# Two z units from the unnormalised input, convolutions ahead of the norms, and the first head's memory copies in another ring

## The chip, the cores and the metric

The kernel runs on one core of one Trainium2 chip. The metric is the device time of one execution in microseconds (us). Before the change it is 1135.06 us, the median of three runs (1134.79 to 1135.84). The trace and its page come from one further execution under the profiler.

## What is computed

One inference step of a one-layer hybrid encoder, for 512 prompt frames of a new stream and 32 sample frames of a running one (544 columns, T, together). Cut to what matters here:

```python
def _rmsnorm(x, g):
    xf = x.astype(jnp.float32)
    y = xf * lax.rsqrt(jnp.mean(xf * xf, axis=-1, keepdims=True) + EPS)
    return (y * g.astype(jnp.float32)).astype(x.dtype)
...
        xn = _rmsnorm(h, norm_g[l])
        proj = xn @ w_in[l]
        u, v_m, z_m, ig_pre, fg_pre, q_h, f_h, i_h, g_h, ga, gb = jnp.split(proj, _split_points(), axis=-1)
        c, conv_new = _causal_conv(u, conv0[l].astype(u.dtype), conv_w[l], conv_b[l])
        c = jax.nn.silu(c).astype(f32)
        ch = c.reshape(B_, T, M_HEADS, M_HD)
        qm = jnp.einsum('bthd,hde->bhte', ch, w_qm[l].astype(f32))
        km = jnp.einsum('bthd,hde->bhte', ch, w_km[l].astype(f32)) * (M_HD ** -0.5)
        vm = v_m.astype(f32).reshape(B_, T, M_HEADS, M_HD).transpose(0, 2, 1, 3)
        ig = (ig_pre.astype(f32) + b_ig[l].astype(f32)).transpose(0, 2, 1)
        lf = jax.nn.log_sigmoid(fg_pre.astype(f32) + b_fg[l].astype(f32)).transpose(0, 2, 1)
        hm, C_new, n_new, m_new = _mlstm(qm, km, vm, ig, lf, C0[l].astype(f32), n0[l].astype(f32), m0[l].astype(f32))
        hm = _head_layernorm(hm.transpose(0, 2, 1, 3), mnorm_g[l].astype(f32))
        hm = (hm + m_skip[l].astype(f32) * c) * jax.nn.silu(z_m.astype(f32))
        ya = hm.astype(x.dtype) @ w_brm[l]
```

An RMS norm multiplies each frame by one number, r, and each input channel by a gain, g. So a product of the input with g alone, scaled by r per frame afterwards, is the product of the normalised input. The mLSTM has four heads of 512 channels each. Behind it come an HGRN2 branch, a merge and the output, which the change does not touch.

## The kernel before

**Numbers and layout.** Channels lie on the 128 partitions, frames along a row. The input is eight tiles x0 to x7 (line 202), each with its 544 columns and the gain. To keep float32 accuracy, each operand of TensorE is a pair: a high part, rounded to the matmul's format on ScalarE, and a low part, the remainder, by a subtraction on VectorE. A product takes three matmuls (high with high, low with high, high with low). For weights this is `split_piece` (line 127): the raw weight arrives by a DMA on SP's queue into one of eight raw buffers, ScalarE casts the high part (line 132), VectorE or, for some weights, POOL subtracts the low part (line 133).

**Two forms of the input.** `x0` (line 1237) holds the pairs of the input times g, without r; they are made first, for the u products that begin the kernel. `xs` (line 1290) holds the pairs of the normalised input: `norm(k)` multiplies x by g and rb in place on VectorE (line 1286) and casts the high part on ScalarE (1289); `norm_low(k)` subtracts on VectorE (1293). `rb` (1297) is r of every frame, on all partitions.

**The first stage (lines 1215 to 1438).** In this block the order of the instructions on ScalarE, VectorE and TensorE is the order of the program. TensorE runs u (four tiles of the first head, from x0), the gate rows, and then the value product (lines 1333 to 1372): eight steps k of twelve matmuls, into four PSUM banks vp, with vq for the sample frames after the steps 3 and 7. Between these steps stand the norms, the weight splits (`value_weight`), and the scaling of u (`conv_scale`). Behind the loop follow, for each of four tiles, the causal convolution: `conv_first` on ScalarE (646), `conv_rest`, three multiply-adds on VectorE (651), `silu` on ScalarE (657, 658, with the cast 1381) and `silu_low` on VectorE (1386). The result is scaled out of vp by `value_out` (1396, 1397). `stage_gates` (714) is a generator: a bias on ScalarE; then line 725 on VectorE with Exp and Ln on ScalarE; then scans along the rows; then further exponentials.

**The pump and the heads (lines 1439 to 1479).** From here only TensorE's order is written out; the instructions of the other engines are placed by a scheduler, by priority, with the pairs `tc.high_priority()` and `tc.issue_after(...)` to steer it. `Pump` hands out further projections in small steps. For the first head these are four z units of class `One` (347), 32 to 35, of 48 matmuls each, from `xs`; then pairs of u units of the next head (class `Two`, line 404), which also read `xf`, sums and differences of the normalised input made by `xf_sums` (320) and laid into the buffers that `x0` leaves (`pair_tile`, tags x0 and x1; q's pairs use them too). `pump.prepare(n)` asks for the loads and splits of the first n blocks; each z unit has four blocks. The first two z units run ahead of the first head's k (`pump.to(EARLY)`, line 1445), z2 and z3 later. A finished z unit is copied out of PSUM by VectorE and goes through Silu on ScalarE (lines 686 and 688).

For each head: `stage_k`, `stage_q`, `stage_scores`, then `mchain` (952). In it `memory` (910) accumulates one of four blocks of the new memory C in a pair of PSUM banks (there are two pairs in all, `paux`), copies it into a tile Co on ScalarE (929) and writes it to HBM. `sample()` (1036) computes the sample frames' numerators, which VectorE adds up (1047). `new_memory` (1023) updates the running stream's memory.

**The rings of buffers.** Tag "s" (`slot`, line 80) has 22 buffers, tag "e" (`eslot`, line 83) has 12. A tile waits until a buffer of its ring is free, that is, until the last reader of the tile in it is done. Co, the tiles x, ub, z, kf and the old memory c0 are in "e"; scores, weighted keys and convolutions are in "s".

## Time and profile before

| | |
|---|---|
| median of three runs | 1135.06 us |
| the profiled execution: its time | 1135.85 us |
| the profiled execution: span from first to last instruction | 1133.3 us |
| TensorE's mean granted clock over the span | 0.995 of full speed |
| instructions | 23757 |
| DMA | 157.94 MB, mean 139 GB/s |

The page gives, for each engine, its busy time and share of the span (PE is TensorE, PEld its weight loads, DVE VectorE, ACT ScalarE, POOL GpSimd, SP the engine that issues most DMAs). The trace can also be asked for a list of waits (who waited for whom), for a table of stages (busy time, granted clock and DMA in given stretches) and for a timeline of each engine. In a timeline's line stand the start and the duration in us, the engine, the line of the kernel, the operation, what it writes and reads, and how many alike were merged; in brackets, how long the engine was idle before it and what it waited for.

### The profile page before, as it was taken

To read this page: it belongs to the slowest core of one execution; us is meant where nothing else is said; L and a number is where in the kernel's file an instruction comes from. 1 tells how busy PE (TensorE), PEld (TensorE's weight loads), DVE (VectorE), ACT (ScalarE), POOL (GpSimd) and SP (SyncE) were. 2 spreads that over 40 slices of the span, in tenths; PEclk is the share of its full clock that TensorE was granted. 3 is DMA by queue.
4 is the path that set the end of the run, shared out by engine and by line. 5 is a ranking of instruction groups with operands and counts; after the bars stand their busy time and mean duration, and the time that the engine had idled before them with its cause. 6 is when DMAs were issued, how large, how long until landed. Compare 5 with 4: busy or idle time off the path is not lost.

```text
span 1133.3 us, 23757 instructions
## 1 busy us (share of the span) xinstructions
PE 1112.4 (98%) x8733; PEld 1088.1 (96%) x8733; DVE 900.9 (79%) x2040; ACT 669.5 (59%) x1506; POOL 163.7 (14%) x308
## 2 busy tenths in 40 slices
PE   8999899999999999999999999999999999999998
PEld 8888799999999999999999999999999999999998
DVE  6898958778598685986888689999999977654485
ACT  6578436755476463765556367776766667333462
POOL 7113000000020000201100123222332210000000
PEclk9999999999999999999999999999999999999999
DMA  7133223414354232453567666666666685332753
GB/s 226 55 114 105 70 93 113 157 60 124 114 162 164 66 122 103 150 174 100 181 194 210 203 140 141 133 152 152 149 142 152 153 220 151 122 101 79 252 160 117
DMA packets 90140, 157.94 MB, mean 139 GB/s; under 512 B 10149, under 2 KB 17829, under 8 KB 90025
## 3 DMA queue, kind: packets, MB, share of 16 engines
q1 hardware_dynamic: 80352, 139.33, 38.4%
q0 software_dynamic: 8784, 15.99, 9.2%
q8 instruction: 68, 1.11, 0.4%
q10 hardware_dynamic: 888, 1.12, 0.3%
q14 instruction: 48, 0.39, 0.1%
HBM read 131.49 MB, written 24.91 MB: 138 GB/s over the span
## 4 chain that ended last, share of the span: by engine, by line
PE 83%; DVE 5%; DMA 3%; ACT 2%; issue 1%; POOL 0%; ACTq 0%; POOLq 0%; DVEq 0%
PE d L502 34%; PE ya L167 8%; PE yb L167 4%; PE q L167 4%; PE o L167 4%; PE pg L1860 4%; PE k L167 4%; PE C L917 4%; PE sc L877 3%; PE nm L1094 3%; PE pl L1632 2%; DMA ws<-in_w_in 2%; PE ple L167 1%; PE yt L1142 1%; PE ht L1708 1%
## 5 line engine op out<-in xcount | busy, mean ns | idle before, releaser
L420 POOL DMA_DIRECT2D ws<-in_w_in x46 | 40.4, 884 | 237.2 <-DVE hkq L1656 54.9
L516 ACT COPY t<-d 128x272 f32<-128x272 f32 x126 | 47.7, 379 | 8.8 <-PE d L502 8.7
L1656 DVE TENSOR_TENSOR hkq<-hkq,q 128x288 f32<-128x288 f32 (+1 forms) x96 | 40.8, 431 | 2.6 <-PE pl L1640 0.9
L1632 PE MATMUL pl<-hkq,km 128*128 128x128 f32 x224 | 38.0, 292 | 1.1 <-ACT km L1621 0.9
L651 DVE SCALAR_TENSOR_TENSOR cv<-ub,vec,cv 128x547 f32<-128x547 f32 x48 | 37.5, 783 | 0.4
L1029 DVE SCALAR_TENSOR_TENSOR c<-c,wi,Cs 128x258 f32<-128x258 f32 x32 | 15.3, 480 | 25.9 <-PE Cs L1027 25.8
L1632 PEld LDWEIGHTS pl<-hkq,km 128*128 128x128 f32 x224 | 31.1, 189 | 3.2 <-ACT km L1621 2.8
L1621 ACT COPY km<-hkq 128x256 f32<-128x256 f32 x56 | 24.0, 428 | 13.9 <-DVE hkq L1656 4.6
L929 ACT COPY Co<-C 128x258 f32<-128x258 f32 x30 | 9.8, 378 | 34.1 <-PE C L917 24.9
L1172 DVE TENSOR_TENSOR y<-ya,y 128x272 f32<-128x272 f32 x48 | 18.9, 435 | 8.7 <-PE ya L167 8.6
L1663 DVE COPY_PREDICATED at<-lmask,pl 128x256 f32<-128x256 uint8 (+1 forms) x56 | 25.3, 451 | 0.1
L1105 ACT COPY y<-nm 128x516 f32<-128x516 f32 x16 | 9.4, 590 | 23.3 <-PE nm L1094 22.8
L643 POOL COPY uo<-ub 128x3 f32<-128x3 f32 x16 | 17.9, 1116 | 36.1 <-DVE ub L525 27.0
L1082 DVE BATCH_NORM_STATS2 bs<-y 128x6 f32<-128x512 f32 (+1 forms) x20 | 13.8, 690 | 8.8 <-ACT y L1105 8.6
L917 PE MATMUL C<-vhl,kwh 128*128 128x258 f32 x96 | 16.5, 296 | 4.4 <-ACT Co L929 3.8
L1600 POOL TENSOR_SCALAR_AFFINE_SELECT aa<-at 128x128 f32<-128x128 f32 x32 | 19.6, 643 | 8.1 <-DVE at L1663 8.0
L817 POOL COPY vsm<-vt 128x96 f32<-128x96 f32 x12 | 7.3, 608 | 87.7 <-DVE vt L523 45.2
L1094 PE MATMUL nm<-vhl,sh 128*128 128x258 f32 x112 | 18.4, 287 | 1.2 <-ACT y L1105 1.2
L477 POOL DMA_DIRECT2D ws<-in_w_in x15 | 15.2, 1014 | 29.3 <-DVE ws272l L133 23.5
L917 PEld LDWEIGHTS C<-vhl,kwh 128*128 128x128 f32 x96 | 14.0, 201 | 4.7 <-ACT Co L929 4.0
L1847 DVE TENSOR_TENSOR h<-o,h 128x272 f32<-128x272 f32 x16 | 6.3, 436 | 14.5 <-PE o L167 14.5
L1094 PEld LDWEIGHTS nm<-vhl,sh 128*128 128x128 f32 x112 | 15.4, 190 | 2.0 <-ACT y L1105 1.7
(4503 smaller groups left out, 4980.4 us busy)
## 6 DMA issues: line engine op xcount, KB each, us to landing
ws<-in_w_in POOLq DMA_DIRECT2D x61, 256.0 KB, 4.9
ws<-in_w_in SPq DMA_DIRECT2D x46, 256.0 KB, 4.1
ya_d<-y SPq DMA_DIRECT2D x32, 272.0 KB, 2.5
y<-ya_d SPq DMA_DIRECT2D x24, 272.0 KB, 3.4
c<-in_C SPq DMA_DIRECT2D x16, 258.0 KB, 3.8
out_Cs<-c SPq DMA_DIRECT2D x16, 258.0 KB, 2.8
out_Cp<-Co SPq DMA_DIRECT2D x12, 258.0 KB, 2.4
x<-in_xT SPq DMA_DIRECT2D x8, 272.5 KB, 4.7
```

The lines of the kernel that those rows point to most:

```text
L167: PE.matmul(both[b][:m, :TH], part(w, off + k * step, m, x), xx[:, half(b)], start=(k == 0 and j == 0), stop=(k == n - 1 and j == 2),)
L420: G.dma_start(t, w_in[u][:, i * WP : (i + 1) * WP], accum_op=ALU.add)
L502: PE.matmul(ps, ww[:, c], xx, start=(start and k == 0 and j == 0), stop=end, skip_group_check=not start,)
L516: self.kept = S.copy(t, ps)
L651: V.scalar_tensor_tensor(cv[:, :547], ub[:, j : j + 547], vcol(V_CW + 4 * ft + j), cv[:, :547], ALU.mult, ALU.add)
L877: PE.matmul(pn[:, 0, :n], ks[f][x][:, j * P : (j + 1) * P], qs[f][y][:, NS + j * P : T], start=(f == 0 and i == 0), stop=(f == KH - 1 and ...
L917: PE.matmul(pn[g][:, :VH], kw[b][x][:, f * P : (f + 1) * P], vv[b][y][:, g * VH : (g + 1) * VH], start=(b == 0 and j == 0), stop=(b == NB ...
L1094: PE.matmul(pn[:, g, :VH], st[j][x][:, (i - j) * P : (i - j + 1) * P], vv[j][y][:, g * VH : (g + 1) * VH], start=(j == 0 and q == 0), stop ...
L1632: PE.matmul(pn[:, 0, b * P : (b + 1) * P], km[:, b * P : (b + 1) * P], view(qq, b * P, ((2 * c, P // (2 * c)), (HB + c, 2), (1, c))), star ...
L1656: V.tensor_tensor(x, x, d, ALU.mult)
L1663: V.copy_predicated(at[:, :n], lmask[:, li, :n], pn[:, 0, :n])
L1860: PE.matmul(ps, part(w, k * P, P, x), xx[:, c], start=(k == 0 and j == 0), stop=(k == KD - 1 and j == 2))
```

## The change

It has these parts.

- `One` takes an optional source. The first two z units of head 0 read `x0` in place of `xs`, and their eviction multiplies by `rb` in place of copying.
- In the first stage the convolutions (scale, first, rest, silu, low) move to before and into the value product; the norms move behind, the last four to after the value evictions. Each value weight's split keeps its rank among the others. `pump.prepare(1)` and `prepare(3)` move into step 2 of the value product, `prepare(5)` and `(7)` stand between the evictions and the last norms. `st8[0]["last"]`, which holds back `xf_sums(0)` and `(3)`, is now the last `norm_low`.
- `stage_gates` asks for its row tiles when they are first written, not at its start.
- Head 0's Co tiles come from ring "s" in place of "e".
- In head 0's `mchain`, `xf_sums(1)` no longer stands ahead of `sample()`; it is issued behind the sample's last sum, with `xf_sums(2)`.
- The u evictions `conv_in` lose their `issue_after` on POOL.

The definitions of `silu`, `silu_low` and `value_out` stand unchanged further up; their old place is cut.

```diff
--- before.py
+++ after.py
@@ -347,9 +347,9 @@
     class One:
 
 
-        def __init__(self, key, unit, cut, then):
+        def __init__(self, key, unit, cut, then, src=None):
             self.key, self.unit, self.cut, self.then = key, unit, cut, then
-            self.ps = None
+            self.ps, self.src = None, src
 
         def raws(self):
             return [(self.unit, 0), (self.unit, 1)]
@@ -381,7 +381,7 @@
                     self.ps = phalves(f"d{self.unit}")
                 halves = (slice(0, self.cut), slice(self.cut, T))
                 for k in (2 * i, 2 * i + 1):
-                    xh, xl = xs[k]
+                    xh, xl = (self.src or xs)[k]
                     for j, (x, xx) in enumerate(((0, xh), (0, xl), (1, xh))):
                         for b, c in enumerate(halves):
                             PE.matmul(
@@ -683,7 +683,10 @@
             z = eslot(f"z{h}{f}")
             for b in range(2):
                 with tc.high_priority():
-                    out = V.tensor_copy(z[:, b * TH : (b + 1) * TH], acc[b][:, :TH])
+                    if f < 2:
+                        out = V.tensor_tensor(z[:, half(b)], acc[b][:, :TH], rb[:, half(b)], ALU.mult)
+                    else:
+                        out = V.tensor_copy(z[:, half(b)], acc[b][:, :TH])
             st8[h].setdefault("copies", []).append(out)
             act = S.activation(z[:, :T], z[:, :T], AF.Silu)
             st8[h]["z"][f] = (z, act)
@@ -704,7 +707,7 @@
             todo += [pair("v", f, 16 + h * KH + f, lambda f: plain(eslot(f"vt{h}{f}")), value) for f in (0, 2)]
             todo += [pair("z", f, 32 + h * KH + f, lambda f: plain(eslot(f"z{h}{f}")), gate) for f in (0, 2)]
         else:
-            todo += [One(("z", f), 32 + f, TH, lambda acc, f=f: gate_one(f, acc)) for f in range(KH)]
+            todo += [One(("z", f), 32 + f, TH, lambda acc, f=f: gate_one(f, acc), x0 if f < 2 else None) for f in range(KH)]
         if h + 1 < MH:
             st8[h + 1]["ub"] = [None] * KH
             todo += [pair("u", f, (h + 1) * KH + f, inner_tile, inner) for f in (0, 2)]
@@ -713,19 +716,20 @@
 
     def stage_gates(fg, ig):
 
-        e, bl, *rr, m, em = (slot(f"row{i}")[:MH, :T] for i in range(KD))
-        lf = wl = e
-        nm = m
         ct = tp.tile([P, T + NS], F32, tag="bc", name="rst")
         rst = ct[:MH, :T]
         ct = tp.tile([P, T + NS], F32, tag="bc", name="d0")
         d0 = ct[:MH, :T]
         S.activation(fg, fg, AF.Identity, bias=gv[:, 1:2])
         yield
+        e = slot("row0")[:MH, :T]
         V.scalar_tensor_tensor(e, fg, -1.0, fg, ALU.mult, ALU.min)
         S.activation(e, e, AF.Exp)
         S.activation(e, e, AF.Ln, bias=1.0)
         yield
+        bl, *rr, m, em = (slot(f"row{i}")[:MH, :T] for i in range(1, KD))
+        lf = wl = e
+        nm = m
         V.scalar_tensor_tensor(lf, fg, 0.0, e, ALU.min, ALU.subtract)
         G.memset(rst, 1.0)
         G.memset(rst[:, 0:1], 0.0)
@@ -923,7 +927,7 @@
                     )
             if b < NB - 1:
                 yield
-        co = eslot(f"Co{h}{f}")
+        co = (eslot if h else slot)(f"Co{h}{f}")
         with tc.high_priority(), tc.issue_after(after.ins) if after is not None else nullcontext():
             for g in range(2):
                 S.copy(co[:, g * VH : (g + 1) * VH], pn[g][:, :VH])
@@ -1015,9 +1019,6 @@
             lo = slice(NS, 2 * NS)
             with tc.high_priority():
                 low = V.tensor_tensor(vs[lo, :HD], pt[lo, 0, :], vs[lo, :HD].bitcast(F32), ALU.subtract)
-        if h == 0:
-            with tc.issue_after(low.ins):
-                xf[1] = xf_sums(1)
         yield 3
 
         def new_memory(f, g):
@@ -1053,7 +1054,8 @@
             ysm, read, last = sample()
             if h == 0:
                 with tc.issue_after(last.ins):
-                    xf[2] = xf_sums(2)
+                    for k in (1, 2):
+                        xf[k] = xf_sums(k)
             yield 1
         if h == MH - 1:
 
@@ -1264,8 +1266,7 @@
         w3.append(split_piece(raws[1], "wu31", WP, WSPLIT))
         wg = gate_weight(a["w_gate"], "wg")
         products(KD - 1)
-        with tc.issue_after(summed.ins):
-            uin = [conv_in(f, acc[f], False) for f in range(NF)]
+        uin = [conv_in(f, acc[f], False) for f in range(NF)]
         acc.append(phalves("u3"))
         steps(acc[3], w3, range(U3AT))
         pb = paux("r0pb")
@@ -1290,23 +1291,52 @@
             xs.append((xh, xl))
 
         def norm_low(k):
-            V.tensor_tensor(xs[k][1], xt[k][:, :T], xs[k][0].bitcast(F32), ALU.subtract)
+            return V.tensor_tensor(xs[k][1], xt[k][:, :T], xs[k][0].bitcast(F32), ALU.subtract)
+
+        cc, cs, vv0 = [], [], []
+
+        def silu():
+            f = len(cc)
+            cc.append(conv_silu(f, cv[f]))
+            hi, lo = slot(f"cs{f}h", F32R), slot(f"cs{f}l", F32R)
+            S.copy(hi[:, :T], cc[f][:, :T])
+            cs.append((hi, lo))
+
+        def silu_low(f):
+            hi, lo = cs[f]
+            V.tensor_tensor(lo[:, :T], cc[f][:, :T], hi[:, :T].bitcast(F32), ALU.subtract)
+
+        def value_out():
+            b = len(vv0)
+            if b < 2:
+                vhl = sp.tile([P, 2, SLOT], F32R, tag="d", name=f"vhl0{b}", bufs=2)
+                vh, vl = vhl[:, 0], vhl[:, 1]
+            else:
+                vh, vl = eslot(f"vh0{b}", F32R), eslot(f"vl0{b}", F32R)
+            c = r[:, b + 1 : b + 2]
+            S.mul(vh[:, :HD], vp[b], c)
+            V.scalar_tensor_tensor(vl[:, :HD], vp[b], c, vh[:, :HD].bitcast(F32), ALU.mult, ALU.subtract)
+            with tc.issue_after(summed.ins):
+                G.tensor_copy(vh[:, HD:VW], one4)
+                G.tensor_copy(vl[:, HD:VW], zero4)
+            vv0.append((vh, vl))
 
         value_weight()
         value_weight()
         rb = slot("rb")
         S.copy(rb[:, NS:T], pb[:, 0, :])
         S.copy(rb[:, :NS], pb[:, 1, :NS])
-        conv_scale(uin[0])
-        norm(0)
-        norm(1)
+        cv = []
+        for f in range(NF):
+            conv_scale(uin[f])
+            cv.append(conv_first(f, uin[f]))
+        conv_rest(0, uin[0], cv[0])
         value_weight()
-        norm(2)
-        norm_low(0)
-        with tc.issue_after(summed.ins):
-            uin.append(conv_in(3, acc[3], True))
-        value_weight()
-        cv = [conv_first(0, uin[0])]
+        uin.append(conv_in(3, acc[3], True))
+        conv_rest(1, uin[1], cv[1])
+        silu()
+        cv.append(conv_first(3, uin[3]))
+        silu_low(0)
         gp = phalves("gates")
         for k in range(KD):
             both = ((GW + GN, x0[k][0]), (GN, x0[k][1]))
@@ -1319,41 +1349,45 @@
                         start=(k == 0 and m > GN),
                         stop=(k == KD - 1 and m > GN),
                     )
-        norm(3)
-        norm_low(1)
-        norm(4)
         gt = slot("gt")
         for b in range(2):
             S.copy(gt[:GN, half(b)], gp[b][:GN, :TH])
             V.tensor_tensor(gt[:GN, half(b)], gp[b][GW : GW + GN, :TH], gt[:GN, half(b)], ALU.add)
         value_weight()
+        conv_rest(2, uin[2], cv[2])
+        silu()
+        silu_low(1)
+        value_weight()
 
         vp = [pd.tile([P, 512], F32, tag="h", name=f"vp{b}") for b in range(NB)]
         vq = paux("vq")
+        pump = Pump(fill(0))
         for k in range(KD):
             if k == 1:
-                norm(5)
-                norm_low(2)
-                norm_low(3)
-                value_weight()
-                norm(6)
-                norm_low(4)
+                conv_rest(3, uin[3], cv[3])
+                silu()
+                silu_low(2)
+                silu()
                 fg, ig = (slot(n)[:MH, :T] for n in ("fg", "ig"))
                 V.tensor_tensor(fg, gt[0:MH, :T], rb[0:MH, :T], ALU.mult)
                 V.tensor_tensor(ig, gt[32 : 32 + MH, :T], rb[32 : 32 + MH, :T], ALU.mult)
-                norm(7)
+                gates = stage_gates(fg, ig)
+                next(gates)
+                value_weight()
+                silu_low(3)
+                norm(0)
+                norm(1)
             if k == 2:
-                norm_low(5)
                 value_weight()
-                norm_low(6)
-                norm_low(7)
-                conv_scale(uin[1])
-                cv.append(conv_first(1, uin[1]))
-                conv_scale(uin[2])
-                cv.append(conv_first(2, uin[2]))
-            if k == 3:
+                norm_low(0)
+                norm_low(1)
+                norm(2)
                 value_weight()
-                cv.append(conv_first(3, uin[3]))
+                norm(3)
+                norm_low(2)
+                pump.prepare(1)
+                norm_low(3)
+                pump.prepare(3)
             wh, wl = wv[k]
             xh, xl = x0[k]
             three = ((xh, wh), (xl, wh), (xh, wl))
@@ -1371,70 +1405,33 @@
                     i = k + 1 - NB + j
                     PE.matmul(vq[j * NS : (j + 1) * NS, 0, :], xg[:, i], wraw[i], start=(i < NB), stop=(i >= NB))
 
-        cc, cs, vv0 = [], [], []
-        gates = stage_gates(fg, ig)
-
...
-        pump = Pump(fill(0))
-        conv_rest(0, uin[0], cv[0])
-        silu()
-        next(gates)
-        conv_rest(1, uin[1], cv[1])
-        silu_low(0)
-        pump.prepare(1)
-        silu()
-        pump.prepare(3)
         value_out()
         value_out()
-        conv_rest(2, uin[2], cv[2])
-        silu_low(1)
-        silu()
-        conv_rest(3, uin[3], cv[3])
+        norm(4)
         value_out()
         value_out()
-        silu_low(2)
-        silu()
+        norm_low(4)
+        norm(5)
         pump.prepare(5)
-        silu_low(3)
-        pump.prepare(7)
-        st8[0]["wk"] = weight(a["w_km"][0, 0], "wk00", eng=G)
         vsum = slot("vsum")[:NS, :HD]
         S.copy(vsum, vq[:NS, 0, :])
         for j in range(1, NB):
             V.tensor_tensor(vsum, vq[j * NS : (j + 1) * NS, 0, :], vsum, ALU.add)
+        pump.prepare(7)
+        st8[0]["wk"] = weight(a["w_km"][0, 0], "wk00", eng=G)
+        norm_low(5)
         vs0 = small("vs", [3 * NS, VW], F32R, bufs=1)
         for i in (0, 2):
             S.mul(vs0[i * NS : (i + 1) * NS, :HD], vsum, r[:NS, 0:1])
-        st8[0]["last"] = V.scalar_tensor_tensor(
+        V.scalar_tensor_tensor(
             vs0[NS : 2 * NS, :HD], vsum, r[:NS, 0:1], vs0[:NS, :HD].bitcast(F32), ALU.mult, ALU.subtract
         )
         with tc.issue_after(summed.ins):
             G.tensor_copy(vs0[:, HD:VW], vone)
+        norm(6)
+        norm(7)
+        norm_low(6)
+        st8[0]["last"] = norm_low(7)
         next(gates)
     with tc.manual_schedule(engines={mybir.EngineType.PE}):
         for h in range(MH):
```

98 lines of the change are left out of this document (49 added, 49 removed).

## The prediction

> **What bounds the kernel now.** I read the page's busy times first, then the list of TensorE's waits over the first 260 us, then the granted clock around the longest of them, then TensorE's timeline there.
>
> ```profile
> PE 1112.4 (98%) x8733; PEld 1088.1 (96%) x8733; DVE 900.9 (79%) x2040; ACT 669.5 (59%) x1506; POOL 163.7 (14%) x308
> ```
>
> TensorE is busy for 1112.4 of the 1133.3 us of the span. The other engines count only where TensorE waits for them, and at most some 21 us of waiting can be had, beside matmuls that run slowly.
>
> ```profile
> PE C L917 <- ACT Co L929: 3.8, 1, 3.8
> PE d L387 <- ACT wi330h L132: 2.5, 1, 2.5
> PE k L167 <- POOL wk010l L133: 1.3, 1, 1.3
> ...
> PE k L167 <- ACT wk010h L132: 1.0, 1, 1.0
> PE nm L1094 <- ACT y L1105: 0.7, 1, 0.7
> ...
> PE C L917 <- DVE y L1047: 0.5, 1, 0.5
> ```
>
> Columns: total, times, longest. Three places hold 8.6 us: the second z unit (2.5), the second half of head 0's k (1.3 and 1.0), the third block of head 0's new memory (3.8). Each costs more than its wait, since TensorE comes back slow:
>
> ```profile
> 74.00:76.00 2.00, 2.00 (x10) 2.00 (x10) 2.00 (x2) 2.00 (x5) 1.77 (x2) 0.50 0.51 130
> ...
> 90.00:92.00 2.00, 2.00 (x9) 2.00 (x10) 2.00 (x6) 1.20 (x3) 2.00 (x3) 0.50 0.48 131
> ```
>
> The third column from the right is the granted clock. It is 0.50 of full speed for some 2 to 3 us behind each wait. So I take a place's whole loss from the timeline (start, duration, instruction):
>
> ```profile
> 70.25 0.41 PE L387 MATMUL d<-xh,wi321l 128*128 128x272 f32 x2
> 73.16 0.82 PE L387 MATMUL d<-xh,wi330h 128*128 128x272 f32 x2 [2.50 <-ACT wi330h L132]
> ...
> 80.57 0.42 PE L167 MATMUL k<-cs0h,wk000h 128*128 128x272 f32 x2
> ...
> 86.36 0.41 PE L167 MATMUL k<-cs3h,wk001l 128*128 128x272 f32 x2
> 87.82 0.52 PE L167 MATMUL k<-cs0h,wk010h 128*128 128x272 f32 x2 [1.05 <-ACT wk010h L132]
> ...
> 96.97 0.41 PE L167 MATMUL q<-cs0h,wq000h 128*128 128x272 f32 x2
> ```
>
> A pair of matmuls follows the last every 0.25 us, so the first z unit ends at 70.50, and the first half of k takes 80.57 to 86.61: 6.04 us for 48 matmuls without a stall. The second z unit has 48 as well, and is over at 80.57. Place A loses 80.57 - 70.50 - 6.04 = **4.03 us**. Place B, the second half of k, loses 96.97 - 86.61 - 6.04 = **4.32 us**.
>
> ```profile
> 137.07 0.28 PE L1027 MATMUL Cs<-vs,kws 96*128 96x258 f32 x1
> ...
> 140.47 0.65 ACT L929 COPY Co<-C 128x258 f32<-128x258 f32 x2 [0.28 <-DMA out_Cs<-c]
> ...
> 141.17 1.23 PE L917 MATMUL C<-vhl,kwh 128*128 128x258 f32 x4 [3.82 <-ACT Co L929]
> ...
> 145.55 0.28 PE L1027 MATMUL Cs<-vs,kws 96*128 96x258 f32 x1
> 145.67 0.64 PE L917 MATMUL C<-vhl,kwh 128*128 128x258 f32 x4
> ...
> 148.56 0.28 PE L1027 MATMUL Cs<-vs,kws 96*128 96x258 f32 x1
> ```
>
> Here the fourth block of the memory runs 145.67 to 148.68, 3.01 us. The third could start at 137.19 and end at 140.20; it ends at 145.67. Place C loses **5.47 us**. What the third block waits for is a PSUM buffer, emptied by a copy into Co at 140.47, and that copy waited for a buffer of Co: the only free one came when c's write-out had landed.
>
> A rule beside this. The Trainium skill, "TensorE: Matmul & The Clock Gate", section "Part 1: The HAM clock gate", has the clock fall only after an idle window of about 3.4 us. The 2.50 us at place A were enough here, so the trace disagrees, and I follow the trace. By the rule A would be worth 2.50 us instead of 4.03.
>
> **The change part by part.** First, place A. Why is wi330h late? ScalarE's timeline:
>
> ```profile
> 69.43 0.61 ACT L658 ACTIVATE c<-cv 128x512 f32<-128x512 f32 x1
> 71.39 0.66 ACT L688 ACTIVATE z<-z 128x544 f32<-128x544 f32 x1 [1.35 <-DVE z L686]
> 71.96 0.63 ACT L1381 CAST cs3h<-c 128x544 fp32r<-128x544 f32 x1
> 72.49 0.61 ACT L132 CAST wi330h<-wi33r 128x512 fp32r<-128x512 f32 x1
> ```
>
> The first z unit's silu (line 688) stood in the queue ahead of the last convolution's cast and of the second z unit's weight cast. It could only run when the first z unit was finished, so the second unit's weights could never be ready when TensorE wanted them. With the change the first two z units need only x0 (there since the u products) and rb at the eviction, so the order can be turned round: the convolutions go beside the value matmuls, the norms behind. The work is the same; what matters is what stands in front of wi330's two halves. I walk VectorE's new order with these durations:
>
> ```profile
> 42.61 1.36 DVE L1293 TENSOR_TENSOR xl<-x,xh 128x544 fp32r<-128x544 f32 x2
> ...
> 62.52 1.41 DVE L1397 SCALAR_TENSOR_TENSOR vhl<-vp,rms_r,vhl 128x512 fp32r<-128x512 f32 x2
> 63.85 2.43 DVE L651 SCALAR_TENSOR_TENSOR cv<-ub,vec,cv 128x547 f32<-128x547 f32 x3
> ...
> 70.57 0.79 DVE L686 COPY z<-d 128x272 f32<-128x272 f32 x2
> ...
> 80.84 0.71 DVE L725 SCALAR_TENSOR_TENSOR row<-fg 4x544 f32<-4x544 f32 x1
> ```
>
> A norm_low is 0.65, a value eviction 0.7, a conv_rest 2.4, a z eviction 0.8 for both halves; I take a norm as a value eviction, 0.7, a weight's low half 0.65, a cast on ScalarE 0.55. From 30.7 on: three conv_scale, conv_rest 0 and 1, u3's eviction, silu_low 0 and the gate additions end near 40.4; conv_rest 2 and 3, wv3 to wv5's splits, three lows, fg, ig and the first two norms end at 52.3; wv6, wv7, two more norms and wi32's split end at 61.4. The two value evictions then end at 63.7, norm 4 at 64.4, the other two value evictions, held up by ScalarE, which runs norm 4's cast first, at 67.0, norm_low 4 and norm 5 at 68.4. ScalarE casts xh5 and then wi330h by 69.4, VectorE has wi330l by 70.1. TensorE wants them at 70.5 and 71.0. So the wait is gone, with **1 us to spare**; wi331l, behind the three additions into vsum and the z eviction, comes at 73.4 against 74.0. Gain 4.03 us; if the cover of 1 us fails by a little, TensorE loses just that.
>
> What must stay hidden: the value matmuls need wv4 to wv7 at these times.
>
> ```profile
> 51.98 0.72 PE L1362 MATMUL vp<-wv4h,x 128*128 128x512 f32 x2
> ...
> 60.47 0.63 PE L1362 MATMUL vp<-wv7h,x 128*128 128x512 f32 x2
> ```
>
> In the walk wv4 is split by 44.7 and wv7 by 57.8, against 51.98 and 60.47 (2.7 us to spare). The z eviction becomes a multiplication by rb; no row has it. The nearest are the copy above, 0.8 for both halves, and norm's line, 0.7 for a whole row: between a gain of 0.1 and a loss of 0.4 on VectorE, hidden by the unit behind it, whose PSUM halves are others. I take the copy's. The z units' write of x4 and x5's buffers waits for norm_low 4 at most, done at 67.7, and for norm_low 5, at 74.1, against 70.6 and 76.6. Each prepare that moves takes its weight loads along, into SP's queue:
>
> ```profile
> 52.06 0.80 SPq L122 DMA_DIRECT2D wi32r<-in_w_in  x2
> ...
> 60.90 1.95 SPq L122 DMA_DIRECT2D wi34r<-in_w_in  x2
> ```
>
> wi32's waits for raw buffers that the last vq of the first half frees just before 52, wi34's for those of wi32, split by 61.4 in the walk and at 62.4 now. Asked for earlier they go at the same times, in the same order, and nothing behind them moves. POOL's copies of uo come up to 16 us earlier, into idle time of POOL. x0's buffers, which q and the sums xf 0 and 3 take over, stay in use until the second z unit ends at 76.5; the sums stand behind norm_low 7, past 77, and q's first write comes some 15 us later, so nothing waits for them.
>
> Second, place B. The queue in front of wk010h:
>
> ```profile
> 80.82 1.28 ACT L726 ACT_TABLE_LOAD   x1
> 82.11 0.66 ACT L726 ACTIVATE row<-row 4x544 f32<-4x544 f32 x1
> 82.79 1.28 ACT L688 ACT_TABLE_LOAD   x1
> 84.08 0.66 ACT L688 ACTIVATE z<-z 128x544 f32<-128x544 f32 x1
> 84.76 1.28 ACT L727 ACT_TABLE_LOAD   x1
> 86.05 0.66 ACT L727 ACTIVATE row<-row 4x544 f32<-4x544 f32 x1
> ```
>
> Exp, the second z's silu, Ln: three table loads. Their start is line 725 on VectorE, ended at 81.55, 1.0 us after k began. In the new order line 725 follows norm_low 7: my walk ends it at 79.1, or 80.4 if wi34's two low halves come first, while k begins at 76.5. The chain then starts 2.6 to 3.9 us after k instead of 1.0. Against it, silu of z can run before Exp and save a table load and itself (1.9 us), or wk010h itself can run while ScalarE waits. So B changes by a loss of 1.9 us (chain late by 2.9, against the 1.0 that k's eviction would wait anyway) up to a gain of all 4.32. I take **0**, since the two shifts nearly cancel.
>
> Third, place C. Counting head 0's slots of ring "s" from the code: eight of kw, six of scores, four of c are alive when the memory runs, 18 of 22. Four Co fit, so no copy waits for a write-out. The copies take 0.65 us a block, against blocks of 3.01, so the PSUM pair turns over. Gain 5.47 us. Moving xf_sums(1) behind the sample's sums frees VectorE between them: the 0.5 us wait for line 1047 should go too. Its transforms were done before 142 and are first read by the pair behind z3, past 166; cover of 20 us. I leave the 0.7 us wait of nm as it is, with a gain of 0.7 at the low end. C in all: **6.0 us**.
>
> The rest (silu_low, gate rows asked for later, weights of k on POOL) moves work beside busy TensorE, and behind 200 us TensorE hardly waits, so the gain reaches the end whole. Sum: 4.03 + 0 + 6.0 = 10.0. The profiled execution took 1135.85 (span 1133.3, and 2.55 around it), 0.79 above the median: 1135.85 - 10.0 = 1125.8, and by the median **1125.0 us**.
>
> **The rivals.**
> (1) The scheduler again sets the first z's silu ahead of wi330h: 1 us of slip does it. Only C pays: 1129.0. For it: it happened now, at the same point. Against: wi330 stands earlier by a conv and three casts.
> (2) B goes as well, wk010h being cast while ScalarE waits for line 725: 1125.0 - 4.3 - 0.7 = 1120.0. For it: by the walk ScalarE idles there 1 to 2 us. Against: its load waits for raw buffers that come free only then.
> (3) Ring "s" is fuller than my count, and a Co waits for the Co before it, as in ring "e": only A pays, 1131.0.
> (4) The change doesn't do what it says: A's wait moves to wi331 or k, C's stays; 1135.
> (5) Slower: the convolutions stand ahead of the value weights. If VectorE falls more than 3 us behind the walk, every weight from wv4 to wv7 comes late, TensorE starves once a step, and the clock, which fell behind waits of 1.05 and 1.30 at B, stays at 0.50. The stretch 51.98 to 63.4 then takes 11.4 more, and the waits 2: 1125.0 + 13.4 = 1138.4.
> (6) Only idle of a whole window gates the clock; then A pays 2.50 and the time is 1126.5. The row 74 to 76 speaks against it; no chance of its own.
>
> **How the numbers follow.** Forecast 0.47 (1122.5 to 1127.5), (1) 0.16, (2) 0.15, (3) 0.10, (4) 0.07, (5) 0.05. About 0.2%, 2.3 us, is what a measurement of this kernel tells from no change. Faster: 0.47 + 0.16 + 0.15 + 0.10 = 0.88; same 0.07; slower 0.05. The range reaches from (2) to just above (3), 1120.0 to 1131.5, and leaves out 0.12.
>
> **What would show it.** A: no wait of TensorE for wi330h, the clock at 1.00 from 66 to 82, k beginning near 76.5. B: a wait for wk010 of some 2 us remains, and 0.50 behind it. C: Co's copies wait for TensorE alone and the four memory blocks follow every 3.0 us. Wrong would be: waits for wv, a wait for cols or for k's PSUM, or a Co that waits for a DMA.

## The result

The changed kernel takes **1126.65 us** (median of five runs, 1126.06 to 1128.63), beside 1135.06 for the kernel before on the same chip (five runs, 1134.77 to 1137.06): a ratio of 0.9926, 95% interval 0.9912 to 0.9941. That is 8.4 us less, where 10.1 were predicted. The profiled execution took 1126.18 us, its span is 1124.3.

First the list of TensorE's waits over the first 260 us of the kernel after (total, times, longest):

```profile
PE k L167 <- POOL wk011l L133: 2.2, 1, 2.2
...
PE k L167 <- ACT wk011h L132: 1.1, 1, 1.1
PE sc L881 <- ACT q L860: 0.9, 1, 0.9
```

The waits for wi330h (2.5), Co (3.8) and y (0.5 and 0.7) are gone, and so are those for the two parts of wk010 (1.0 and 1.3). In their place stand waits for wk011, the other piece of k's second weight half (1.1 and 2.2, together more than the two of wk010), one for the scores' q, and one for the low part of wi330. Now TensorE's timeline of the kernel after, at the points that divide the stages:

```profile
62.09 0.77 PE L387 MATMUL d<-x,wi320h 128*128 128x272 f32 x4
...
69.74 0.52 PE L387 MATMUL d<-x,wi330l 128*128 128x272 f32 x2 [0.85 <-DVE wi330l L133]
...
75.38 0.41 PE L167 MATMUL k<-cs0h,wk000h 128*128 128x272 f32 x2
...
81.40 0.42 PE L167 MATMUL k<-cs0h,wk010h 128*128 128x272 f32 x2
...
84.19 0.52 PE L167 MATMUL k<-cs2h,wk011h 128*128 128x272 f32 x2 [1.12 <-ACT wk011h L132]
...
87.20 0.82 PE L167 MATMUL k<-cs2h,wk011l 128*128 128x272 f32 x2 [2.24 <-POOL wk011l L133]
...
93.96 0.42 PE L167 MATMUL q<-cs0h,wq000h 128*128 128x272 f32 x2
...
126.61 0.64 PE L1042 MATMUL nm<-c,qw 128*32 128x258 f32 x8
...
148.90 0.41 PE L387 MATMUL d<-xh,wi350h 128*128 128x272 f32 x2
```

and the rows of the kernel before that the prediction didn't show; below them the start of rb's copy on ScalarE, before and then after:

```profile
64.36 0.52 PE L387 MATMUL d<-xh,wi320h 128*128 128x272 f32 x2
...
128.12 0.64 PE L1041 MATMUL nm<-c,qw 128*32 128x258 f32 x8
...
157.35 0.41 PE L387 MATMUL d<-xh,wi350h 128*128 128x272 f32 x2
```

```profile
29.97 0.59 ACT L1298 COPY rb<-r0pb 128x512 f32<-128x512 f32 x1 [0.21 <-PE r0pb L248]
```

```profile
28.16 0.59 ACT L1327 COPY rb<-r0pb 128x512 f32<-128x512 f32 x1 [0.21 <-PE r0pb L248]
```

Differences of such starts give the stages, in us. The first row is the start of rb's copy; z3 begins where its matmuls run without a break (three pairs of it come earlier, behind the sample); the last column is the best kernel found (all4, below).

| stage | before | after | gained | all4 |
|---|---|---|---|---|
| start to rb | 29.97 | 28.16 | 1.81 | 28.36 |
| rb to first z unit | 34.39 | 33.93 | 0.46 | 34.31 |
| two z units (place A) | 16.21 | 13.29 | 2.92 | 12.68 |
| k (place B) | 16.40 | 18.58 | -2.18 | 13.83 |
| q, scores, to the sample | 31.15 | 32.65 | -1.50 | 31.50 |
| sample, memory, to z3 (place C) | 29.23 | 22.29 | 6.94 | 22.22 |
| the rest | 975.95 | 975.40 | 0.55 | 975.30 |
| span | 1133.30 | 1124.30 | 9.00 | 1118.20 |

A and C gained, C more than forecast and A less; k lost, q and the scores lost; and 1.8 us came from a stretch that the prediction had not priced at all. The rest, 975 us, varied from 974.4 to 978.0 between the profiles of this study, so its 0.55 says nothing. The table compares one profile with one, and the z units and k vary between profiles of the same code as well: the part on rb, below, compares several.

**Place C** did what was said. The Co tile's view, before and then after, says what ScalarE stood idle for ahead of the copies (us, times):

```profile
  DMA out_Cp<-Co: 6.5, 3
```

```profile
  PE C L921: 4.4, 4
```

No copy waits for a write-out any more, only for the matmuls. The last matmuls of the four blocks start 3.02 to 3.03 us apart:

```profile
131.79 0.28 PE L1028 MATMUL Cs<-vs,kws 96*128 96x258 f32 x1
...
134.82 0.28 PE L1028 MATMUL Cs<-vs,kws 96*128 96x258 f32 x1
...
137.84 0.28 PE L1028 MATMUL Cs<-vs,kws 96*128 96x258 f32 x1
...
140.87 0.28 PE L1028 MATMUL Cs<-vs,kws 96*128 96x258 f32 x1
```

**Place A** kept 0.85 us. VectorE's timeline after:

```profile
68.30 0.79 DVE L687 TENSOR_TENSOR z<-d,rb 128x272 f32<-128x272 f32 x2 [1.59 <-PE d L387]
69.01 0.68 DVE L133 TENSOR_TENSOR wi330l<-wi33r,wi330h 128x512 fp32r<-128x512 f32 x1
```

and ScalarE's:

```profile
67.30 0.62 ACT L132 CAST wi330h<-wi33r 128x512 fp32r<-128x512 f32 x1
...
76.11 0.62 ACT L132 CAST wk010h<-wk01r 128x512 fp32r<-128x512 f32 x1
...
78.88 1.28 ACT L727 ACT_TABLE_LOAD   x1
...
81.12 1.28 ACT L728 ACT_TABLE_LOAD   x1
...
83.54 0.60 ACT L132 CAST wk011h<-wk01r 128x512 fp32r<-128x512 f32 x1
```

wi330h was cast in time, but VectorE's queue has the first z unit's eviction ahead of wi330l, and stood idle 1.59 us for it. It is rival (1) in small, on another engine. **Place B**: the first piece of k's second weight half, wk010, was cast at 76.11, ahead of Exp, as in rival (2); the other piece, wk011, came only behind Exp and Ln (two table loads), at 83.54, and then POOL took 2.87 us for its low part. The clock fell to 0.50 behind these waits (third column from the right; a row of the kernel after's table of stages):

```profile
88.00:90.00 2.00, 2.00 (x11) 2.00 (x10) 2.00 (x4) 0.69 (x2) 0.39 (x2) 0.50 0.82 258
```

### The profile page after: what moved, and what is told of

Read it like the earlier page. It is cut to its first block, busy times and chain, and to the rows that moved or that the text cites. A ratio compares the mean times of both kernels' runs of the same rounds, so it can differ in the third digit from the quotient of the medians.

```text
span 1124.3 us, 23764 instructions
## 1 busy us (share of the span) xinstructions
PE 1110.2 (99%) x8733; PEld 1086.6 (97%) x8733; DVE 898.3 (80%) x2040; ACT 670.7 (60%) x1505; POOL 165.3 (15%) x308
## 3 DMA queue, kind: packets, MB, share of 16 engines
q8 instruction: 68, 1.11, 0.4%
q10 hardware_dynamic: 888, 1.12, 0.3%
## 4 chain that ended last, share of the span: by engine, by line
PE 90%; DVE 4%; DMA 3%; ACT 1%; issue 1%; POOL 1%; SPq 0%; ACTq 0%; POOLq 0%; DVEq 0%
PE d L502 36%; PE ya L167 8%; PE yb L167 4%; PE o L167 4%; PE pg L1857 4%; PE k L167 4%; PE q L167 4%; PE C L921 4%; PE nm L1096 3%; PE sc L881 3%; PE pl L1629 2%; PE vp L1396 2%; PE u L287 2%; DMA ws<-in_w_in 2%; PE d L387 1%
## 5 line engine op out<-in xcount | busy, mean ns | idle before, releaser
L1629 PEld LDWEIGHTS pl<-hkq,km 128*128 128x128 f32 x224 | 31.1, 189 | 2.2 <-ACT km L1618 1.9
L933 ACT COPY Co<-C 128x258 f32<-128x258 f32 x30 | 9.8, 378 | 31.8 <-PE C L921 29.5
L895 ACT CAST sh<-dm 128x512 fp32r<-128x512 f32 (+3 forms) x16 | 7.4, 461 | 17.2 <-DVE dm L889 17.1
L821 POOL COPY ksm<-kf 128x96 f32<-128x96 f32 x16 | 8.5, 532 | 60.7 <-ACT kf L834 60.7
L1759 ACT ACTIVATE osq<-kq 128x128 f32<-128x128 f32 x32 | 9.8, 307 | 12.4 <-DVE kq L1754 12.1
```

Source lines behind the costliest of these rows:

```text
L1629: PE.matmul(pn[:, 0, b * P : (b + 1) * P], km[:, b * P : (b + 1) * P], view(qq, b * P, ((2 * c, P // (2 * c)), (HB + c, 2), (1, c))), star ...
```

## The experiments

All times are medians, the ratios against runs of the kernel before on the same chip, with 95% intervals. The experiments ran on four chips, so the ratios compare better than the times. Four questions: which half pays, what the x0 source itself is worth, what holds k, and what happened before rb.

**Which half pays.** c_only is the kernel before with the two edits of the memory; first_only is the kernel after without them; co_only is the first of the two edits alone.

```diff
-        co = eslot(f"Co{h}{f}")
+        co = (eslot if h else slot)(f"Co{h}{f}")
...
-        if h == 0:
-            with tc.issue_after(low.ins):
-                xf[1] = xf_sums(1)
...
-                    xf[2] = xf_sums(2)
+                    for k in (1, 2):
+                        xf[k] = xf_sums(k)
```

> Only the memory part of the change: Co of head 0 in ring s, xf_sums(1) behind the sample's sums; the first stage is that of before. By the traces of before and after, the stretch from the sample's first matmul to the last nm matmul fell from 29.16 to 22.29 us, 6.9 us. Theory: that is all of the change's gain that lasts, so 1128.2 (1127.2 to 1129.2), and the four memory blocks follow every 3.0 us with no Co waiting for a DMA. Rival (the first stage carries part of the gain): 1129.5 or more.

> Only the first stage of the change: z from x0, convolutions ahead of the norms; Co back in ring e and xf_sums(1) back ahead of the sample. Theory: the second z unit gains 3.0 us and the value part 0.3, the second half of k loses 2.2 more than before, and the scores 1.4, so the sum is about 0: 1134.8 (1133.8 to 1136). Rival: the 1.8 us by which the profiled run of after was ahead before any changed instruction belong to the change: 1133.0. Second rival: the first stage gains its 3 us whole: 1131.7.

> The kernel before with one edit only: head 0's Co comes from ring s instead of ring e. Theory (Co's buffer is the whole of place C): the 3.8 us wait of C for Co goes, with the slow clock behind it, 5.5 us of the 1135.06: about 1129.6. The 0.5 us wait for y (line 1047 on VectorE) stays. Rival (the moved sums xf_sums(1) carry part of it, since they stand on VectorE between the sample's sums and the state): 1131 to 1132, and a wait of C for DVE or of nm for y that grows.

Measured: c_only 1129.28 us, ratio 0.9936 (0.9921 to 0.9951); first_only 1134.03, ratio 0.9982 (0.9970 to 0.9994); co_only 1131.26, ratio 0.9960 (0.9948 to 0.9973). The halves, 6.5 and 1.7 us against their own runs of before, add up to 8.2 of the 8.4: they don't hinder each other. From the sample to z3, c_only takes 22.29 us, like the kernel after, and co_only 23.18 instead of 29.23: the ring is worth 6.05 and the moved sums 0.89. In co_only a wait of 0.6 at the second block stays where before one for y stood. By its time (3.5 us) co_only comes out with the rival; by its stage, where the 5.5 expected are 6.05, with the theory. I go by the stage, since the sum of the two, 6.94, is what c_only and the kernel after show as well.

The surprise is first_only. Its two z units take 13.28 us, all of place A's gain, and yet little of it arrives: k takes 17.47 and q to the sample 34.65, 1.07 and 3.50 more than before. What arrives turns out below to come from something else.

**What x0 itself is worth.** z_norm is the kernel after, but its first two z units read `xs` and are copied out plainly; the order of convolutions and norms stays.

```diff
-                    if f < 2:
-                        out = V.tensor_tensor(z[:, half(b)], acc[b][:, :TH], rb[:, half(b)], ALU.mult)
-                    else:
-                        out = V.tensor_copy(z[:, half(b)], acc[b][:, :TH])
+                    out = V.tensor_copy(z[:, half(b)], acc[b][:, :TH])
...
-            todo += [One(("z", f), 32 + f, TH, lambda acc, f=f: gate_one(f, acc), x0 if f < 2 else None) for f in range(KH)]
+            todo += [One(("z", f), 32 + f, TH, lambda acc, f=f: gate_one(f, acc)) for f in range(KH)]
```

> The kernel after, but the first two z units read the normalised input and their eviction is a plain copy: the convolutions stay ahead of the norms. Theory (the unnormalised source is what allows this order): the first z unit waits for the norms of pieces 4 to 7, whose last low part ended at 79.3 in the kernel after, against a first z unit from 62.2 to 68.2: the z units end some 8 to 11 us later, of which k, whose weights are then early, gives back 3: 1132 to 1136. Rival (the order of the convolutions alone is what pays): 1126 to 1128.

Measured: 1128.56 us, ratio 0.9948 (0.9931 to 0.9964). The first z unit waits for the norms as the theory says; z_norm's timeline:

```profile
72.44 0.82 PE L387 MATMUL d<-xl,wi321h 128*128 128x272 f32 x2 [4.12 <-DVE xl L1291]
...
86.13 0.41 PE L167 MATMUL k<-cs0h,wk000h 128*128 128x272 f32 x2
...
98.18 0.41 PE L167 MATMUL q<-cs0h,wq000h 128*128 128x272 f32 x2
```

The z units take 23.66 us, 10.4 longer than in the kernel after. But k takes 12.05 instead of 18.58, since its weights are then ready, and q to the sample 0.7 less: the sample begins only 3.5 us later. I had given k back 3 us; it was 6.5, with the slow clock. So 10 us of waiting for the norms cost 1.9 us at the median: what TensorE wins ahead of k it waits for again in k. The 1.9 us are an estimate at best: the two intervals overlap, and the profiled execution of z_norm was the slowest of its four (1132.28).

**What holds k.** The ring of high parts (`split_piece`, tag "wh") has five buffers. In the kernel after, when wk011 wants one, wk000, wk001, wk010 and the third z unit's wi340 and wi341 have them. wi34 is split long before its use, because the pump runs ahead. limit stops the pump ahead of wi34 until q is done. gates_early moves line 726 with Exp and Ln (725 before) into step 2 of the value product. p5 splits wi330, the first piece of wi33, before the second pair of value evictions. wk_v makes the low parts of k's second half on VectorE in place of POOL.

```diff
 limit
+                pump.limit = 8
...
+                pump.limit = None
+                pump.prepare(12)
 gates_early
+                next(gates)
...
-        next(gates)
 p5
+        pump.prepare(5)
...
-        pump.prepare(5)
 wk_v
-            w = st8[h].pop("wk", None) or weight(a["w_km"][h, u], f"wk{h}{u}", eng=V if h else G)
+            w = st8[h].pop("wk", None) or weight(a["w_km"][h, u], f"wk{h}{u}", eng=V)
```

> The kernel after, but the splits of the third z unit (wi34) are held back until q's second half, so that they take none of the five buffers for high parts while k runs. Theory W: wk011's cast waited for one of these five (held by wk000, wk001, wi340, wi341, wk010) until k's first half let wk000 go, and only so fell behind Exp and Ln on ScalarE. Then both casts of wk01 stand ahead of Exp, the waits of k for wk011 (1.1 and 2.2 us) and the slow clock behind them go, 6.5 us at most; the gate rows' chain, which then comes late for cols or scores, may take back 1 to 3: 1121 to 1124. Rival T (ScalarE's queue with its table loads is the cause, not the buffers): wk011's cast stays behind Ln, 1126 to 1127.

> The kernel after, but line 725's subtraction with Exp and Ln runs in the third step of the value product, so that no table load for them stands among k's casts; the buffers are as in after. Theory W: wk011's cast still cannot start before k's first half has let wk000 go, some 4.5 us after k begins, and ScalarE waits there; it then comes 3 us earlier than in after, the waits of k shrink to under 1 us and the clock stays up: 1120.5 to 1123. Rival T: the cast follows wk010's at once, 1 us after k's begin, and no wait is left. Against both: the Silu table must be loaded once more ahead of the first z's silu, and the value weights wv7 come late, a new wait of TensorE in the value product: 1126 or more.

> The kernel after with one edit: wi33's split is prepared ahead of the second pair of value evictions, so wi330l stands ahead of the first z's eviction on VectorE. Theory (the 0.85 us wait left at the second z unit is only the order of these two instructions): the wait for wi330l is 0, k starts about 0.9 earlier after the first z unit's start (12.4 instead of 13.2), and the time is 1125.8 if k's second half keeps its length. Rival (k's second half is bound by wk011, which Exp and Ln and the release of a buffer hold): k's waits grow by what was won, 1126.6.

> The kernel after with one edit: the low parts of k's second weight half (wk010l, wk011l) are subtracted on VectorE, not on POOL. Theory (of the two waits in k's second half, 1.12 for wk011h and 2.24 for wk011l, about half of the second is made by POOL: its subtraction took 2.87 us there, against 1.30 for wk010l, while VectorE ran a scan, wq000l and line 738 beside it, and line 738 took 1.77): on VectorE wk011l takes 0.65 behind the scan and ends near 86.1 instead of 87.15, the wait for it falls from 2.24 to about 1.1, line 738 takes 0.7 to 0.8, k from first to second half's end is 1 to 2 us shorter (18.6 to about 17.2) and the time is 1125.3. Rival (the release of the buffer and the Exp and Ln in front of wk011h are all of it, POOL nothing): the wait for the low part stays near 2 behind VectorE's own queue, 1126.6. Second rival (VectorE is full there, and what it now does late are the gate rows): sc waits longer for q, 1127 to 1128.

| | time, us | ratio | two z units | k | q to sample |
|---|---|---|---|---|---|
| after | 1126.65 | 0.9926 (0.9912 to 0.9941) | 13.29 | 18.58 | 32.65 |
| limit | 1126.72 | 0.9917 (0.9903 to 0.9931) | 13.28 | 16.12 | 34.52 |
| gates_early | 1128.23 | 0.9929 (0.9915 to 0.9943) | 17.35 | 12.57 | 35.93 |
| p5 | 1125.26 | 0.9918 (0.9903 to 0.9932) | 12.42 | 16.14 | 34.84 |
| wk_v | 1122.92 | 0.9889 (0.9873 to 0.9906) | 13.28 | 14.83 | 32.91 |

limit freed the buffer: wk011h was cast at 76.48 and no weight of k was late. gates_early took Exp and Ln away: wk011h was still cast only at 85.29, when wk000h's last matmuls, begun at 84.80, were over. So the late wk011h has both causes, buffer and queue. Neither edit won time. TensorE's waits in limit, then in gates_early:

```profile
PE k L167 <- ACT kf L834: 2.1, 2, 1.9
PE q L167 <- DVE q L861: 1.7, 1, 1.7
```

```profile
PE sc L881 <- ACT q L860: 2.6, 1, 2.6
PE d L387 <- DVE wi331l L133: 2.3, 1, 2.3
```

With the weights there, k waits for its PSUM, emptied by kf's copies that stand behind the same Exp and Ln; with Exp and Ln early, the gate rows' scans come between the additions into vsum, wi331l is late, and the scores wait for q. p5 removed its wait (12.42, as expected) and met kf and q next. Its 1.4 us lie inside the intervals. Each wait had covered another. In limit, p5 and gates_early a slow clock is part of what q and the scores take longer: it was at 0.50 from 102 to 104 in limit and from 100 to 102 in p5, and at 0.54 from 112 to 114 in gates_early, while in the kernel after it stayed at 1.00 from 94 to the sample.

wk_v is the exception, and gained more than I had expected (3.7 us by the medians, 1.3 expected). TensorE's timeline in wk_v, then VectorE's, then the table of stages:

```profile
84.14 0.52 PE L167 MATMUL k<-cs2h,wk011h 128*128 128x272 f32 x2 [1.11 <-ACT wk011h L132]
...
86.03 0.52 PE L167 MATMUL k<-cs2h,wk011l 128*128 128x272 f32 x2 [1.12 <-DVE wk011l L133]
```

```profile
85.32 0.65 DVE L133 TENSOR_TENSOR wk011l<-wk01r,wk011h 128x512 fp32r<-128x512 f32 x1
85.90 0.77 DVE L738 SCALAR_TENSOR_TENSOR row<-ig,vec,row 4x544 f32<-4x544 f32 x1
```

```profile
86.00:88.00 2.00, 1.97 (x15) 1.97 (x16) 2.00 (x6) 0.69 (x2) 0.59 (x2) 1.00 0.45 121
```

The wait for the low part fell from 2.24 to 1.12, as forecast, and the clock stayed at 1.00, which I had not counted. That is no accident of one profile: the mean granted clock was 1.000 in all four executions of wk_v, and 0.997 or 0.998 in all five of the kernel after. The kernel after shows what made POOL slow: first POOL's row, then VectorE's beside it.

```profile
84.28 2.87 POOL L133 TENSOR_TENSOR wk011l<-wk01r,wk011h 128x512 fp32r<-128x512 f32 x1
```

```profile
84.11 1.34 DVE L737 TENSOR_TENSOR_SCAN row<-rst,row 4x544 f32<-4x544 f32 x1
85.37 0.65 DVE L133 TENSOR_TENSOR wq000l<-wq00r,wq000h 128x512 fp32r<-128x512 f32 x1
85.95 1.77 DVE L738 SCALAR_TENSOR_TENSOR row<-ig,vec,row 4x544 f32<-4x544 f32 x1
```

POOL's subtraction, 1.30 us for wk010l, ended 1.13 after VectorE's wq000l (87.15 against 86.02); VectorE's line 738, 0.77 in wk_v, ended 0.57 after POOL's. By these rows the two take turns. The Trainium skill, "SBUF — State Buffer", section "SBUF: two separate sides", says that VectorE instructions with two inputs from SBUF and GpSimd instructions that read SBUF share one pair of ports, which the one that starts first holds for its whole instruction while the other stands still. The trace agrees in these durations; on who goes first see the last section.

**What happened before rb.** No product, weight or norm ahead of rb had been touched, so I first took the 1.81 us for scatter. But in all seven profiles I then had with the first half of the change rb began at 28.1 to 29.0, in all three without it at 29.5 to 31.1. One edit reaches there: the making of u's buffers lost its `issue_after`, which lets POOL's small copies into ub go ahead of its second addition of squares. sum_back undoes that edit alone in the kernel after, sum_only makes it alone in the kernel before; only POOL's order changes.

```diff
 sum_only
-        with tc.issue_after(summed.ins):
-            uin = [conv_in(f, acc[f], False) for f in range(NF)]
+        uin = [conv_in(f, acc[f], False) for f in range(NF)]
```

> The kernel after with one edit undone: the making of u's buffers stands again behind the sum of squares on POOL (issue_after summed, line 1267 of the kernel before). On VectorE, ScalarE and TensorE no instruction changes its place, on POOL the second addition of squares (128x544) and the products xg go ahead of the small copies into ub again. Theory (the 1.8 us that the profile of the kernel after has won before rb come from this order on POOL: in the kernel before that addition runs at 11.59 to 12.92, beside wf2l on VectorE, which takes 1.86 us; in the kernel after wf2l takes 0.55): wf2l takes 1.8 again, TensorE waits 1.25 us for it, rb's copy starts at 29 to 30, and the time is 1126.65 + 1.5 = 1128.1. Rival (the 1.8 us are scatter between profiles, by when the first loads land): 1126.6 and a rb anywhere from 28 to 30.

> The kernel before with that one edit alone: the making of u's buffers no longer waits for the sum of squares, which moves six small copies on POOL ahead of the second addition and of the products xg, and changes no other engine's order. Theory (as for sum_back): wf2l takes 0.55, no wait of TensorE for it, rb's copy starts near 28.5, the time is 1135.06 - 1.5 = 1133.5. Rival (scatter): 1135, wf2l as in the kernel before in some runs and not in others.

Measured: sum_back 1127.83 us, ratio 0.9941 (0.9924 to 0.9957), rb at 29.52; sum_only 1133.41, ratio 0.9987 (0.9977 to 0.9997), rb at 27.92. Both came within 0.3 us of the theory. sum_back's interval overlaps that of the kernel after, so there the rows decide, not the time. VectorE's and POOL's rows, of sum_back (first two fences) and of the kernel after:

```profile
11.03 1.85 DVE L133 TENSOR_TENSOR wf2l<-wf2r,wf2h 128x384 fp32r<-128x384 f32 x1
```

```profile
11.12 1.33 POOL L1251 TENSOR_TENSOR r0q<-r0q,r0q 128x544 f32<-128x544 f32 x1
```

```profile
10.96 0.55 DVE L133 TENSOR_TENSOR wf2l<-wf2r,wf2h 128x384 fp32r<-128x384 f32 x1
```

```profile
15.13 1.35 POOL L1251 TENSOR_TENSOR r0q<-r0q,r0q 128x544 f32<-128x544 f32 x1
```

The same subtraction takes 1.85 us beside POOL's addition and 0.55 without; in sum_back it ends 0.43 after POOL's (12.88 against 12.45). TensorE waited 1.25 us for it in the kernel before. In all fourteen profiles of this study it goes with the edit: 0.55 or 0.56 us with it, 1.85 or 1.86 without. And sum_only alone gains 1.55 us against its runs of before, nearly all of first_only's 1.7: place A's gain was spent in k and at the scores.

Two comparisons bear that out. sum_back is c_only with the new first stage but without the edit on POOL, and the ratios of the two, 0.9941 and 0.9936, can't be told apart. And several profiles share one order of the first stage from rb on; their stages, in us:

| first stage of | profiles | two z units | k | q to sample | the three together |
|---|---|---|---|---|---|
| before | before, c_only, co_only, sum_only | 16.21, 15.15, 16.58, 16.45 | 16.40, 18.69, 16.08, 16.26 | 31.1 to 31.2 | 63.8 to 65.0 |
| after | after, first_only, sum_back | 13.29, 13.28, 13.28 | 18.58, 17.47, 17.92 | 32.6 to 34.7 | 63.8 to 65.4 |

Place A's gain is 1.9 to 3.3 us and the loss at q and the scores at least 1.4, whichever profiles are compared. k's loss, 1.1 by the means, is not clear of the scatter. Together the three stages gained nothing.

**All at once.** all4 is the kernel after with limit, gates_early, p5, and `pump.prepare(7)` ahead of the sums into vsum. all5 is all4 with the gate rows' scans behind the second z's eviction (`copies[1]` for `copies[0]`).

> The kernel after with four edits of order: the third z unit's weights are split only when q is done (their buffers go to wk011), wi33's split stands ahead of the second pair of value evictions and its other half ahead of the sums into vsum, and the gate rows' minimum, Exp and Ln come beside the value matmuls. Theory (what is left in the kernel after are three waits of order, each with its own price): the second z unit has no wait (0.85), k has none (18.58 becomes about 12.2, 6.4), q waits for nothing new: 1126.65 - 7 = 1119.5. Rival (k's gain moves the wait to q and the scores, as in the two single edits, which came out at 1126.7 and 1128.2): a wait of sc for q of 1 to 3 us and of q for its PSUM, 1123 to 1126.

> The kernel of all4 with one more edit of order: the gate rows' scans on VectorE stand behind the second z's eviction instead of the first's. Theory (the only wait that all4 has left around k, 1.3 us for the second z's eviction behind two scans, and the slow clock behind it, is this order): that wait goes, k is 12.1 us instead of about 14, and the time is 1120.56 - 2 = 1118.5. Rival (the scans come 6 us later, and with them the gate rows' way through memory to the scores): the wait turns up as a wait of sc for q on ScalarE of 1 to 2.5 us, 1119.5 to 1121.5.

Measured: **all4 1120.56 us, ratio 0.9872 (0.9859 to 0.9884)**, faster than both kernels; all5 1125.55, ratio 0.9916 (0.9900 to 0.9931). all4's waits that the kernel after has not are 1.3 us of k for the second z's eviction and twice 0.3 of the first z unit for vhl. Its mean granted clock was 1.000 in all four executions. The moved `prepare(7)` was not run alone. all5 removed the 1.3 us, and lost 5 us. TensorE's wait in all5:

```profile
PE sc L881 <- ACT q L860: 2.6, 1, 2.6
```

ScalarE's timeline in all5, then in all4:

```profile
105.05 0.97 ACT L810 ACTIVATE dm<-dm,col 128x128 f32<-128x128 f32 x3
...
106.31 0.38 ACT L860 CAST q<-q 128x272 fp32r<-128x272 f32 x1
```

```profile
103.61 0.70 ACT L810 ACTIVATE dm<-bc,col 128x128 f32<-128x128 f32 x2
...
104.26 0.41 ACT L860 CAST q<-q 128x272 fp32r<-128x272 f32 x1
104.55 0.72 ACT L810 ACTIVATE dm<-dm,col 128x128 f32<-128x128 f32 x2
```

q's last cast stands behind all decay exponentials (line 810) in all5, and between them in all4. From q to the sample all5 takes 35.91 us and all4 31.50; part of that is the clock, which in all5 stood at 0.50 from 108 to 110. The rival had the place right and its price too low. all4 with wk_v's edit was not run.

## Why the prediction came out as it did

The time lay inside the range, 1.65 us from the forecast, but that is in part luck, a sum of errors of both signs: 10.0 = 4.03 + 0 + 6.0 was predicted for the profiled execution, and the stages gave 2.92 - 2.18 + 6.94 = 7.7 there, with 1.81 + 0.46 + 0.55 gained and 1.50 lost elsewhere.

- **Place A**, gain 4.03 with "1 us to spare": the mechanism held (no wait for wi330h, clock 1.00 up to 82, k at 75.38 where 76.5 was said, though 2.27 of that lead was won ahead of the z units), the term measured 2.92. The step that failed was the place of wi330l in VectorE's walk: the z eviction went ahead of it, and p5 gives 0.87 back when that is turned round. The 4.03 itself held a draw of the clock: c_only waits the same 2.50 us for wi330h, its clock stays at 1.00, and its two z units take 15.15 us, not 16.21.
- **Place B**, "I take 0, since the two shifts nearly cancel": a loss of 2.18 in these two profiles, just outside the bound of 1.9, and of 1.1 by the means of several. The walk looked at wk010h alone. That was early, as rival (2) had it; but the second half needs wk011 too, for which no buffer was free, and whose low part shared POOL and VectorE's time with the scans: 3.36 us of waiting in place of 2.35. wk_v shows 3.75 us of k for that low part, slow clock included.
- **Place C**, 6.0: 6.94. The ring paid 6.05 where 5.47 was said, the moved sums 0.89 where 0.5 was; the wait of nm for y (0.7), put at the low end of the range, went too. The count of ring "s" was right; rival (3) fell.
- **The rest** "moves work beside busy TensorE": wrong twice. The edit of one line on POOL won 1.2 to 1.55 us at the start (sum_back, sum_only, by the medians), and at the scores 1.50 were lost, 0.89 of it a wait for q.
- Rivals (1), (4) and (5) did not come: value weights were never late. Rival (6), at 1126.5, lies next to the measured time by chance: the clock did fall behind 1.12 and 2.24 us of waiting in k, and where the second z unit waits for nothing (p5) the stage is 3.79 shorter than before, not 2.50. Yet against c_only, whose clock stayed up there, p5's stage is 2.73 shorter, close to that rival's 2.50: it deserved a chance of its own.

## What to carry to other kernels

A wait that goes is worth its own length only if what TensorE reaches earlier is ready earlier too: list what the next stage needs (buffers, table loads, queues) at its new start before the gain is booked, for every piece of its weights and not the first alone. Where two engines share work in time, compare one instruction's duration with and without the other beside it; a removed ordering on a small engine can be worth more than the edit it came with. Several single repairs may each show nothing and together show 6 us, when each wait covers the next. And before a stage's loss is booked from one profile, look at the same stage in other profiles of the same code: here k differed by up to 2.6 us without any change to it.

## What was not expected of the hardware

VectorE and POOL stand still for each other: 1.85 us instead of 0.55 for a 128x384 subtraction, 2.87 instead of 1.30 for one on POOL. In the first two rows of sum_back, above, VectorE was recorded as starting first (11.03 against 11.12), and still POOL ended first, so the recorded starts don't tell which of the two goes first.

The clock's fall does not follow from the length of the waits alone. In k's second half 1.05 and 1.30 us of waiting (before), 0.67 and 1.30 (co_only) and 1.12 and 2.24 (after) led to 0.50; 1.11 and 1.12 (wk_v) led to none. At the second z unit 2.50 us led to 0.50 in before, co_only and sum_only, and to none in c_only, whose TensorE timeline and table of stages show:

```profile
72.73 0.52 PE L387 MATMUL d<-xh,wi330h 128*128 128x272 f32 x2 [2.50 <-ACT wi330h L132]
```

```profile
74.00:76.00 2.00, 2.00 (x18) 2.00 (x17) 1.97 (x3) 1.89 (x4) 2.00 (x2) 1.00 0.37 131
```

Executions of one kernel differ too: p5's mean granted clock lay between 0.995 (1127.39 and 1128.14 us) and 1.000 (1123.83 and 1124.91 us). What decides a single fall stays open. What the runs show is its worth: 1.1 us less waiting made k 3.75 us shorter in wk_v, where the clock did not fall, than in the kernel after, and 2.6 to 3.75 shorter than in the three profiles of that order.
